# A masked softmax bound by DMA: the first store waits for the last whole load

**Chip and metric.** One core of one Trainium2 chip. The metric is the device time of one execution in microseconds (us). All runs compared here are with a granted clock of 1.0.

## The reference

For each of 16 batches, a softmax over the last axis of 8 x 256 rows, of which only the first `length` columns count; the others become 0. Lengths lie between 128 and 255. The reference, shortened:

```python
# x: (16, 8, 256, 256) float32, lengths: (16,) int32
for b in range(batch):
    masked = x[b, :, :, :lengths[b]]
    masked = masked - np.max(masked, axis=-1, keepdims=True)
    e = np.exp(masked)
    result[b, :, :, :lengths[b]] = e / np.sum(e, axis=-1, keepdims=True)
```

## The kernel before

A batch is 2 MB: 128 partitions of 16 rows of 256 floats, so 16 KB contiguous per partition. There are eight slots in SBUF. SyncE loads batches 0 to 3 whole. GpSimd (POOL in the profile) loads batches 4 to 15, each only as wide as its length needs (widths in steps of 8 columns from 160 to 240, or all 256). VectorE (DVE) clips the columns past the length (the clip uses `len_s`, the bounds on all partitions), ScalarE (ACT) exponentiates and sums, DVE divides, and SyncE stores in pieces. All stores and the four whole loads go through SyncE's queue, called q1 in the profile; GpSimd's loads go through q0.

```python
for h in range(2):                                   # SyncE: batch 0 in two halves
    s = slice(h * half, (h + 1) * half)
    nc.sync.dma_start(out=xt[:, 0, s], in_=x_f[0, :, s]).then_inc(s_ld[h], 16)
nc.scalar.dma_start(out=word64, in_=lengths[None, :]).then_inc(s_word, 16)
for b in range(1, ahead):                            # ahead = 4: batches 1 to 3
    nc.sync.dma_start(out=xt[:, b], in_=x_f[b]).then_inc(s_ld[b + 1], 16)
for b in range(batch):
    for s in parts(b):                               # pieces of a batch: halves and quarters, late ones whole
        nc.sync.wait_ge(s_out, 2 * b + (s.stop - 1) // half + 1)
        # ... (from batch 2 on: an earlier store of the same parity is done)
        nc.sync.dma_start(out=out_f[b, :, s, :], in_=xt[:, b % slots, s, :]) # ...
# ...
nc.gpsimd.dma_start(out=word64_p, in_=lengths[None, :]).then_inc(s_word_p, 16)
# ...
nc.gpsimd.wait_ge(s_v, 1)
for b in range(ahead, slots):                        # the fills: zeros past column 160
    nc.gpsimd.memset(xt[:, b, :, low:], 0.0).then_inc(s_fill, 1)
nc.gpsimd.wait_ge(s_word_p, 16)
nc.gpsimd.wait_ge(s_fill, slots - ahead)
nc.gpsimd.wait_ge(s_ld[ahead - 1], 16)               # GpSimd's gate: batch 2 has landed
with nc.Fori(0, (batch - ahead) // 2, 1, engines=[POOL]) as q:
    # ... two narrow loads a turn: length to a register, branches to its width, issue
```

The softmax here doesn't subtract the row's maximum and nothing guards it: scores larger than these inputs give would overflow.

Of the kernel before, what the change touches and what calls it, by code (L numbers as in the profile page):

```python
# [11 lines left out]
I32 = mybir.dt.int32  # L12
# [4 lines left out]
POOL = mybir.EngineType.Pool  # L17
# [3 lines left out]
def kernel(  # L21
# [6 lines left out]
    nc = tc.nc  # L28
    P = nc.NUM_PARTITIONS

    batch, heads, seq_q, seq_k = x.shape
# [10 lines left out]
    ahead = 4  # L42
# [7 lines left out]
    def parts(b):  # L50


        if b < 10:
            cuts = [0, half, half + quarter, nt]
        elif b < 12 or b == batch - 1:
            cuts = [0, half, nt]
        else:
            cuts = [0, nt]
        return [slice(i, j) for i, j in zip(cuts, cuts[1:])]

    pool = ctx.enter_context(tc.tile_pool(name="all", bufs=1))
    psum = ctx.enter_context(tc.tile_pool(name="psum", bufs=1, space=bass.MemoryType.PSUM))
    xt = pool.tile([P, slots, nt, seq_k], F32, name="xt")
    word64 = pool.tile([1, batch], mybir.dt.int64, name="word64")
    word = word64.bitcast(I32)
    word64_p = pool.tile([1, batch], mybir.dt.int64, name="word64_p")
    word_p = word64_p.bitcast(I32)
    len_b = pool.tile([1, batch], BF16, name="len_b")
    ones = pool.tile([1, P], BF16, name="ones")
    len_f = psum.tile([P, batch], F32, name="len_f")  # L70
# [8 lines left out]
    with tc.tile_critical(no_gpsimd_drain=True):  # L79
        sem = lambda n: ctx.enter_context(nc.semaphore(n))  # L80
        s_word = sem("s_word")
        s_word_p = sem("s_word_p")
        s_ones = sem("s_ones")
        s_lenb = sem("s_lenb")
        s_lenf = sem("s_lenf")
        s_ld = [sem(f"s_ld{k}") for k in range(ahead + 1)]
# [6 lines left out]
        s_v = sem("s_v")  # L93
# [4 lines left out]
        def length(engine, at):  # L98

            return nc.values_load(  # L100
                at,
                engines=[engine],
                skip_runtime_bounds_check_because="compared with constants, never an address",
            )


        for h in range(2):
            s = slice(h * half, (h + 1) * half)
            nc.sync.dma_start(out=xt[:, 0, s], in_=x_f[0, :, s]).then_inc(s_ld[h], 16)  # L109
        nc.scalar.dma_start(out=word64, in_=lengths[None, :]).then_inc(s_word, 16)  # L110
        for b in range(1, ahead):
            nc.sync.dma_start(out=xt[:, b], in_=x_f[b]).then_inc(s_ld[b + 1], 16)  # L112
        for b in range(batch):
            s_b = s_st[b % 2]
            for s in parts(b):
                nc.sync.wait_ge(s_out, 2 * b + (s.stop - 1) // half + 1)
                if b >= 2 and s.start == 0:
                    nc.sync.wait_ge(s_b, 64 * (b // 2 + 1))
                nc.sync.dma_start(
                    out=out_f[b, :, s, :], in_=xt[:, b % slots, s, :]  # L120
                ).then_inc(s_b, 16 * ((s.stop - s.start) // quarter))
# [5 lines left out]
        def pick(v, n, slot, par, ws):  # L127

            if len(ws) == 1:
                w = ws[0]  # L130
                nc.gpsimd.dma_start(  # L131
                    out=xt[:, slot, :, :w], in_=x_n[:, n, :, :w]
                ).then_inc(s_sw[par], 16)
                return
            m = (len(ws) - 1) // 2
            with nc.gpsimd.If(v <= ws[m]):  # L136
                pick(v, n, slot, par, ws[: m + 1])
            with nc.gpsimd.Else():
                pick(v, n, slot, par, ws[m + 1 :])
# [3 lines left out]
            iota_i, pattern=[[1, seq_k]], base=0, channel_multiplier=0  # L143
        ).then_inc(s_iota, 1)
        nc.gpsimd.memset(ones, 1.0).then_inc(s_ones, 1)  # L145
        nc.gpsimd.dma_start(out=word64_p, in_=lengths[None, :]).then_inc(s_word_p, 16)  # L146
        for par in range(2):
            nc.gpsimd.memset(seed[:, par : par + 1], 0.0).then_inc(s_st[par], 64)  # L148
        nc.gpsimd.wait_ge(s_v, 1)
        for b in range(ahead, slots):  # L150
            nc.gpsimd.memset(xt[:, b, :, low:], 0.0).then_inc(s_fill, 1)  # L151
        nc.gpsimd.wait_ge(s_word_p, 16)
        nc.gpsimd.wait_ge(s_fill, slots - ahead)
        nc.gpsimd.wait_ge(s_ld[ahead - 1], 16)
        with nc.Fori(0, (batch - ahead) // 2, 1, engines=[POOL]) as q:  # L155
            for par in range(2):
                n = 2 * q + (ahead + par)
                v_len = length(POOL, word_p[0:1, bass.ds(2 * n, 1)])
                with nc.gpsimd.If(q >= 1):  # L159
                    nc.gpsimd.wait_ge(s_sw[par], 16 * q)  # L160
                    nc.gpsimd.wait_ge(s_st[par], 64 * q)  # L161
                pick(v_len, bass.ds(n, 1), bass.ds(n % slots, 1), par, widths + [seq_k])
# [9 lines left out]
        def step(ins):  # L172
# [8 lines left out]
                out=down, in0=iota_i, scalar1=0.5, scalar2=-big, op0=ALU.add, op1=ALU.mult  # L181
# [7 lines left out]
                out=len_s, in0=len_f, scalar1=big, scalar2=None, op0=ALU.mult  # L189
# [56 lines left out]
        with nc.Fori(0, 2 * batch, 1, engines=[ACT]) as i:  # L246
            nc.scalar.wait_ge(s_min, i + 1)
            at = bass.ds(i % (2 * slots), 1)
            for j in range(half):
                e = x_h[:, at, j, :]  # L250
                ins = nc.scalar.activation(  # L251
                    out=e, in_=e, func=EXP, accum_out=sum_h[:, bass.ds(i, 1), j]
# [32 lines left out]
```

## Time and profile before

| | before |
|---|---|
| time, median of the first 3 runs | 157.06 us (156.97 to 157.08) |
| span of the profiled run | 155.5 us |
| bytes moved | 62.08 MB |
| DVE, ACT busy | 77%, 68% |

The lines that carry the reading are in the prediction below. In short: the 16 DMA engines are busy from 2 us to about 153 (9 tenths in every slice but the first and the last), so a change counts by the DMA time that it wastes or saves. A row of the view of stretches has the stretch and its length in us, the busy time and count of PE, PEld, DVE, ACT and POOL, the granted clock, the DMA share and the GB/s moved.

```profile
2.00:36.00 34.00, 0.17 (x1) 0.10 (x1) 29.88 (x20) 24.41 (x119) 7.61 (x9) 1.00 1.00 402
```

### The profile page before, as it was taken

To read this page: it belongs to the slowest core of one execution; us is meant where nothing else is said; L and a number is where in the kernel's file an instruction comes from. 1 tells how busy PE (TensorE), PEld (TensorE's weight loads), DVE (VectorE), ACT (ScalarE), POOL (GpSimd) and SP (SyncE) were. 2 spreads that over 40 slices of the span, in tenths; PEclk is the share of its full clock that TensorE was granted. 3 is DMA by queue.
4 is the path that set the end of the run, shared out by engine and by line. 5 is a ranking of instruction groups with operands and counts; after the bars stand their busy time and mean duration, and the time that the engine had idled before them with its cause. 6 is when DMAs were issued, how large, how long until landed. Compare 5 with 4: busy or idle time off the path is not lost.

```text
span 155.5 us, 1320 instructions
## 1 busy us (share of the span) xinstructions
PE 0.2 (0%) x1; PEld 0.1 (0%) x1; DVE 120.0 (77%) x84; ACT 105.1 (68%) x514; POOL 19.4 (12%) x26
## 2 busy tenths in 40 slices
PE   0000000000000000000000000000000000000000
PEld 0000000000000000000000000000000000000000
DVE  4963999999999968939895999997977999920000
ACT  3029599999989893956969298989592989400000
POOL 7900031003020202002020202020100000000000
DMA  4999999999999999999999999999999999999991
GB/s 116 428 443 426 434 312 388 416 442 427 393 395 410 415 416 406 420 410 413 409 412 419 402 417 406 415 411 405 425 421 432 420 419 432 457 426 422 415 434 61
DMA packets 10452, 62.08 MB, mean 399 GB/s; under 512 B 930, under 2 KB 1026, under 8 KB 7122
## 3 DMA queue, kind: packets, MB, share of 16 engines
q1 hardware_dynamic: 6336, 41.95, 65.9%
q0 software_dynamic: 4112, 20.12, 32.0%
q14 instruction: 2, 0.02, 0.0%
q10 hardware_dynamic: 2, 0.00, 0.0%
HBM read 28.51 MB, written 33.55 MB: 399 GB/s over the span
## 4 chain that ended last, share of the span: by engine, by line
DMA 67%; DVE 11%; issue 6%; POOLq 2%; SPq 1%; POOL 0%; DVEq 0%
DMA xt<-in_x_dram 60%; DVE xt L224 7%; DMA out_dram<-xt 7%; DVE xt L197 3%; POOLq L100 1%; POOLq L136 1%; POOLq L131 1%; SPq L109 1%; DVE inv_sum L221 0%; POOL xt L131 0%; SPq L112 0%; POOLq L159 0%; POOLq L155 0%; DVEq L214 0%; POOLq L161 0%
## 5 line engine op out<-in xcount | busy, mean ns | idle before, releaser
L251 ACT ACTIVATE xt<-xt x256 | 102.4, 402 | 27.2 <-DVE xt L197 27.2
L224 DVE TENSOR_TENSOR xt<-xt,inv_sum 128x2048 f32<-128x2048 f32 x32 | 73.3, 2292 | 1.1
L251 ACT ACTIVATION_READ_ACCUMULATOR xt<-xt x256 | 48.2, 188 | 0.0
L197 DVE SCALAR_TENSOR_TENSOR xt<-down,len_s,xt 128x2048 f32<-128x2048 f32 (+1 forms) x17 | 37.7, 2222 | 11.1 <-DMA xt<-in_x_dram 10.2
L131 POOL DMA_DIRECT2D xt<-in_x_dram x12 | 12.7, 1057 | 89.7 <-issue 45.7
L221 DVE RECIPROCAL inv_sum<-row_sum 128x8 f32<-128x8 f32 x32 | 6.2, 195 | 2.4 <-ACT xt L251 2.4
L185 DVE CAST len_b<-word 1x16 bf16<-1x16 int32 x1 | 5.6, 5595 | 0.4 <-DMA word<-in_lengths_dram 0.4
L151 POOL MEMSET xt<- 128x1536 f32 x4 | 5.3, 1392 | 0.0
L243 ACT ACT_TABLE_LOAD x1 | 1.3, 1283 | 1.6 <-SPq L79 1.6
L180 DVE TENSOR_SCALAR down<-iota_i 128x256 f32<-128x256 int32 x1 | 0.3, 295 | 1.6 <-POOL iota_i L142 1.6
L146 POOL DMA_DIRECT2D word_p<-in_lengths_dram x1 | 0.6, 643 | 0.1
L188 DVE TENSOR_SCALAR len_s<-len_f 128x16 f32<-128x16 f32 x1 | 0.2, 174 | 0.4 <-PE len_f L167 0.4
L142 POOL IOTA iota_i<- 128x256 int32 x1 | 0.3, 331 | 0.6 <-SPq L79 0.6
L243 ACT ACTIVATE warm<-const-float32-0.0 128x1 f32<-128x1 f32 x1 | 0.2, 203 | 0.0
L145 POOL MEMSET ones<- 1x128 bf16 x1 | 0.2, 194 | 0.0
L167 PE MATMUL len_f<-len_b,ones 1*128 1x16 bf16 x1 | 0.2, 168 | 8.0 <-DVE len_b L185 8.0
L269 POOL MEMSET const-float32-0.0<- 128x1 f32 x1 | 0.1, 98 | 0.3 <-issue 0.3
L148 POOL MEMSET seed<- 1x1 f32 x2 | 0.1, 88 | 0.0
L167 PEld LDWEIGHTS len_f<-len_b,ones 1*128 1x128 bf16 x1 | 0.1, 98 | 8.0 <-issue 8.0
L269 POOL MEMSET const-float32-1.0<- 128x1 f32 x1 | 0.1, 98 | 0.0
L269 POOL MEMSET const-bfloat16-1.0<- 128x1 bf16 x1 | 0.1, 98 | 0.0
L269 POOL MEMSET const-uint8-127<- 128x1 uint8 x1 | 0.1, 98 | 0.0
(1 smaller groups left out, 0.0 us busy)
## 6 DMA issues: line engine op xcount, KB each, us to landing
out_dram<-xt SPq DMA_DIRECT2D x16, 1024.0 KB
out_dram<-xt SPq DMA_DIRECT2D x20, 512.0 KB
xt<-in_x_dram SPq DMA_DIRECT2D x3, 2048.0 KB, 16.0
out_dram<-xt SPq DMA_DIRECT2D x3, 2048.0 KB
xt<-in_x_dram POOLq DMA_DIRECT2D x3, 1728.0 KB, 15.9
xt<-in_x_dram POOLq DMA_DIRECT2D x2, 2048.0 KB, 16.0
xt<-in_x_dram POOLq DMA_DIRECT2D x2, 1600.0 KB, 14.5
xt<-in_x_dram POOLq DMA_DIRECT2D x2, 1280.0 KB, 13.6
```

Source lines behind the costliest of these rows:

```text
L100: return nc.values_load(at, engines=[engine], skip_runtime_bounds_check_because="compared with constants, never an address",)
L109: nc.sync.dma_start(out=xt[:, 0, s], in_=x_f[0, :, s]).then_inc(s_ld[h], 16)
L131: nc.gpsimd.dma_start(out=xt[:, slot, :, :w], in_=x_n[:, n, :, :w]).then_inc(s_sw[par], 16)
L136: with nc.gpsimd.If(v <= ws[m]):
L146: nc.gpsimd.dma_start(out=word64_p, in_=lengths[None, :]).then_inc(s_word_p, 16)
L151: nc.gpsimd.memset(xt[:, b, :, low:], 0.0).then_inc(s_fill, 1)
L185: nc.vector.tensor_copy(out=len_b, in_=word[:, ::2]).then_inc(s_lenb, 1)
L197: return nc.vector.scalar_tensor_tensor(out=t, in0=down[:, None, lo:hi].to_broadcast([P, s.stop - s.start, hi - lo]), scalar=len_s[:, b : ...
L221: step(nc.vector.reciprocal(out=inv_sum[:, b, s], in_=row_sum[:, b, s]))
L224: nc.vector.tensor_tensor(out=t, in0=t, in1=inv_sum[:, b, s, None].to_broadcast([P, half, seq_k]), op=ALU.mult,).then_inc(s_out, 1)
L243: nc.scalar.activation(out=warm, in_=nc.const_aps.tensor(0.0, (P, 1), F32), func=EXP)
L251: ins = nc.scalar.activation(out=e, in_=e, func=EXP, accum_out=sum_h[:, bass.ds(i, 1), j])
```

## The change

Its intent: let the whole loads have the DMA engines to themselves, and let GpSimd's narrow loads be open before the first store is. In passing, GpSimd reads the lengths from the copy that ACT's queue fetches, and the fills wait until DVE has made the bounds. The diff, shortened:

```diff
-        nc.scalar.dma_start(out=word64, ...)         # moved ahead of the loads; same queue of ACT
+        nc.sync.wait_ge(s_ld[ahead], 16)             # ahead of the loop of stores: the hold
-        nc.gpsimd.dma_start(out=word64_p, ...)       # and word64_p, s_word_p with it
-        nc.gpsimd.wait_ge(s_v, 1)
+        nc.gpsimd.wait_ge(s_v, 2)                    # fills after the bounds
-        nc.gpsimd.wait_ge(s_word_p, 16)
+        nc.gpsimd.wait_ge(s_word, 16)
-                v_len = length(POOL, word_p[...])
+                v_len = length(POOL, word[...])
```

More of the change, by code (lines that the diff above doesn't have):

```diff
@@ L65 @@
     word = word64.bitcast(I32)
-    word64_p = pool.tile([1, batch], mybir.dt.int64, name="word64_p")
-    word_p = word64_p.bitcast(I32)
     len_b = pool.tile([1, batch], BF16, name="len_b")
@@ L81 @@
         s_word = sem("s_word")
-        s_word_p = sem("s_word_p")
         s_ones = sem("s_ones")
@@ L104, in length @@
             )
+        nc.scalar.dma_start(out=word64, in_=lengths[None, :]).then_inc(s_word, 16)
         for h in range(2):
@@ L109 @@
             nc.sync.dma_start(out=xt[:, 0, s], in_=x_f[0, :, s]).then_inc(s_ld[h], 16)
-        nc.scalar.dma_start(out=word64, in_=lengths[None, :]).then_inc(s_word, 16)
         for b in range(1, ahead):
             nc.sync.dma_start(out=xt[:, b], in_=x_f[b]).then_inc(s_ld[b + 1], 16)
+        nc.sync.wait_ge(s_ld[ahead], 16)
         for b in range(batch):
@@ L145 @@
         nc.gpsimd.memset(ones, 1.0).then_inc(s_ones, 1)
-        nc.gpsimd.dma_start(out=word64_p, in_=lengths[None, :]).then_inc(s_word_p, 16)
         for par in range(2):
             nc.gpsimd.memset(seed[:, par : par + 1], 0.0).then_inc(s_st[par], 64)
-        nc.gpsimd.wait_ge(s_v, 1)
+        nc.gpsimd.wait_ge(s_v, 2)
         for b in range(ahead, slots):
             nc.gpsimd.memset(xt[:, b, :, low:], 0.0).then_inc(s_fill, 1)
-        nc.gpsimd.wait_ge(s_word_p, 16)
+        nc.gpsimd.wait_ge(s_word, 16)
         nc.gpsimd.wait_ge(s_fill, slots - ahead)
@@ L157 @@
                 n = 2 * q + (ahead + par)
-                v_len = length(POOL, word_p[0:1, bass.ds(2 * n, 1)])
+                v_len = length(POOL, word[0:1, bass.ds(2 * n, 1)])
                 with nc.gpsimd.If(q >= 1):
```

## The prediction

Its sum came to +0.85 us, and so to 157.9 us. Three figures in it are estimates and not readings of a trace: the 0.1 us of the cast, the 0.2 us for the start, and the chance of one in two.

> **What bounds the kernel now.** I read the page first, for what is full. Its line of slices says that DMA is.
>
> ```profile
> span 155.5 us, 1320 instructions
> ...
> DMA  4999999999999999999999999999999999999991
> GB/s 116 428 443 426 434 312 388 416 442 427 393 395 410 415 416 406 420 410 413 409 412 419 402 417 406 415 411 405 425 421 432 420 419 432 457 426 422 415 434 61
> ...
> q1 hardware_dynamic: 6336, 41.95, 65.9%
> q0 software_dynamic: 4112, 20.12, 32.0%
> ```
>
> Every slice but the first and last is at 9 tenths, while DVE is busy 77% of the span and ACT 68%. Queue q1 carries SyncE's four whole loads and all stores (41.95 MB), q0 GpSimd's narrow loads (20.12 MB). The kernel moves 62.08 MB whatever the order, so its time is bytes over rate, plus every stretch in which the 16 engines move nothing. One slice stands out: the sixth, 19.4 to 23.3 us, at 312 GB/s. The view of stretches cuts it finer; the last two columns are the DMA share and GB/s.
>
> ```profile
> 4.00:20.00 16.00, 0.17 (x1) 0.10 (x1) 12.31 (x9) 7.28 (x36) 3.87 (x3) 1.00 1.02 433
> 20.00:21.00 1.00, 0.00 (x0) 0.00 (x0) 1.00 (x1) 1.00 (x7) 0.28 (x1) 1.00 1.34 426
> 21.00:22.00 1.00, 0.00 (x0) 0.00 (x0) 1.00 (x2) 1.00 (x6) 0.92 (x1) 1.00 1.19 279
> 22.00:23.00 1.00, 0.00 (x0) 0.00 (x0) 1.00 (x1) 1.00 (x7) 0.00 (x0) 1.00 0.57 197
> 23.00:24.00 1.00, 0.00 (x0) 0.00 (x0) 0.97 (x3) 1.00 (x6) 0.51 (x1) 1.00 0.73 270
> 44.00:116.00 72.00, 0.00 (x0) 0.00 (x0) 62.91 (x45) 57.79 (x286) 8.67 (x9) 1.00 1.02 412
> 123.00:147.00 24.00, 0.00 (x0) 0.00 (x0) 13.85 (x10) 10.34 (x52) 0.00 (x0) 1.00 1.02 433
> ```
>
> Pure loads run at 433, the mixture of narrow loads and stores at 412, pure stores at 433. From 21 to 24 the three rows sum to 0.746 MB where 433 GB/s would have moved 1.299: 0.553 MB, or 1.3 us, is lost there. I call this **the dip**. Compute has no say at the end: the last DVE operation starts at 134.7 and takes 2.3 us, and stores go on to about 153.
>
> Who holds whom at the changeover is in the timeline (start, duration, engine, line) and in the DMA view of 24.0 to 25.5 and 25.5 to 27.0 us.
>
> ```profile
> 2.30 5.59 DVE L185 CAST len_b<-word 1x16 bf16<-1x16 int32 x1 [0.40 <-DMA word<-in_lengths_dram]
> 2.54 5.33 POOL L151 MEMSET xt<- 128x1536 f32 x4
> 9.29 2.48 DVE L197 SCALAR_TENSOR_TENSOR xt<-down,len_s,xt 128x1024 f32<-128x1024 f32 x2 [0.87 <-DVE len_s L188]
> 16.73 19.80 SPq L119 DMA_DIRECT2D out_dram<-xt  x9
> 20.71 1.20 POOL L131 DMA_DIRECT2D xt<-in_x_dram  x1 [12.85 <-issue]
> ```
>
> ```profile
> q1 hardware_dynamic: 75, 0.61, 98.5%
> ```
>
> ```profile
> q1 hardware_dynamic: 77, 0.37, 59.5%
> q0 software_dynamic: 48, 0.23, 37.1%
> ```
>
> The first store is issued at 16.73, but batch 3, the last whole load, lands only at 24.2 (issued at 3.3, longest landing 20.9 us). From 16 to 19 us the DMA view counts 95 packets, 16 of them tiny, and 1.29 MB: 16 KB a packet, the size of a whole load's row. From 24.0 to 25.5 it is 0.61 MB in 75 packets, 8 KB each, the row of a half store. So the early store did not share the engines with batch 3; it stood behind it and followed without a gap. No q0 packet shows before 25.5, though GpSimd issued at 20.71: its first narrow load needed about 5 us to open. At the changeover it is thus the queued stores that keep the engines fed.
>
> [...] Here the first load, issued at 1.13, shows data at 2.1, which is 1.0 us; and GpSimd's took 5 us. [...] a cast of 1x16 elements takes 5.59 us and ends with the four fills.
>
> **The change part by part.**
>
> *Fills after the bounds.* `word` has landed at 2.30; without fills beside it I expect the cast to take some 0.1 us, and matmul and scaling (0.17 and 0.17 us, with the 0.35 us wait between cast and scaling seen now) to end near 3. The fills (5.33 us) move to about 3.0 to 8.4, still far from GpSimd's gate on batch 2 at 18.5. The first clip can start when batch 0's first half is there (issue 1.13 plus 5.1, the shortest landing: 6.2) instead of 9.29: up to 3 us earlier for DVE and ACT. On the path: nothing, for the stores stand behind batch 3 anyway.
>
> *Lengths shared.* It removes one GpSimd issue (0.64 us) and a few bytes of DMA, both ahead of a 10 us idle stretch of GpSimd: 0 on the path. One doubt: DMA is also slow from 2 to 4 us (246 GB/s, where 433 would be 0.75 MB more in 2 us). Most of that is start-up, but the removed DMA is issued just then; if it does harm, up to half a microsecond comes back.
>
> *The hold.* SyncE now issues its first store only after batch 3's semaphore. Loads before it do not go faster, as no store was among them. After it comes a **hole**: semaphore at 24.2, issue some 0.05 us later (DVE ended at 16.70 and SyncE issued at 16.73 in the old trace), 1.0 us to data: about 25.3. GpSimd's gate (batch 2) and its way to the issue are unchanged, so q0 opens near 25.3 to 25.7 and doesn't fill it. What the old kernel moved of stores before 25.3: from 21 to 24 the view counts 58 large packets and 0.75 MB, which is 34 of 16 KB and 24 of 8 KB, so 0.20 MB of stores; from 24.0 to 25.3 it is 1.3 us of 0.415 MB, 0.54 MB. Together 0.74 MB, at 433 GB/s **1.7 us**, and no later stage can win it back, since the engines are full to the end. The backlog at the release is no problem: with compute earlier, batch 0 and half of batch 1 are ready by then.
>
> *The dip.* This I can't place from one trace. It starts 0.4 us after GpSimd's first narrow issue (20.71) and lasts past the store issues at 21.4 and 21.8, so either may be its cause. If it is GpSimd's opening, it stays; if it is stores standing in the same ring behind reads, the hold takes it away and wins 1.3 us back.
>
> Sum: +1.7 for the hole, minus 1.3 times one chance in two, minus some 0.2 for the start: +0.85 us, so 157.9.
>
> **Rivals.**
>
> 1. *The hole is filled by narrow loads.* The intent: GpSimd is open when SyncE stops. For it: its gate passes 5.7 us before batch 3 lands[...]. Against it: 2.2 us of register work and branches to the issue, and 5 us to the first packet. If q0 opened by 23.9, there would be no hole: 156.9 with the dip, 155.6 without.
> 2. *The dip stays, and the hole comes on top*, with no gain at the start: 158.8. For it: the dip begins before the stores of 21.4 are issued, and the one of 16.73 did no harm for four microseconds. Against it: GpSimd's later issues, 36.24 or 87.15, come with no dip (403 GB/s from 87 to 91).
> 3. *DVE becomes the bound after the release*, as stores start late and slots come free later. From 24 to 44 us DVE is busy nearly all the time. Against it: it starts up to 3 us earlier, the narrow loads pace themselves one behind the other, and the stores end 15 us after the last compute. Worth under 0.5 us.
> 4. *The hold lets more loads be pure* and saves on the mixture (412 against 433). Against it: those rates go with small packets and not with direction, and no packet changes its size: 0.
>
> **Range and chances.** Dip gone, start better, hole partly filled: 156.3. Dip kept, hole whole, and a second stumble of half a microsecond to a microsecond at the release: 159.6. Faster by 2% would need 153.9, that is the dip, the whole start-up loss and more, with no hole: 3 in 100. Slower by 2% would need 160.2, twice the hole: 4 in 100. Within 2%: 93 in 100.
>
> **What would show it.** Right: the cast near 0.1 us and the first clip near 6.3; the first store issued just after batch 3 lands; no packets, or very few, for 1 to 2 us after that; rates of 412 and 433 in the same later stages; an end shifted by the same amount. It is wrong if narrow packets show before batch 3 has landed, if loads of batch 3 land much earlier than 24.2 less the dip, or if the later mixture runs at another rate than 412. If the dip is at the same place, GpSimd's opening is its likely cause; if it is gone, the queued stores.

## The result, and the profile after

The changed kernel takes 157.84 us (median of 4 runs, 157.59 to 158.22), the kernel before 157.01 in the same rounds. The ratio is 1.0055, with a 95% interval of 1.0034 to 1.0076: the same within 2%, but slower beyond the noise. A ratio here is the mean time of one kernel's fast runs over that of the other's of the same rounds, so not quite the ratio of the medians.

The page after, its span and its two DMA lines in 40 slices:

```profile
span 155.9 us, 1320 instructions
...
DMA  4999989999999999999999999999999999999992
GB/s 109 425 450 433 420 341 287 407 434 414 405 395 419 408 424 404 412 417 402 420 415 411 411 403 419 406 415 414 415 445 421 411 429 431 441 425 446 414 427 105
```

There are now two low slices, 341 and 287, where one stood at 312. The stretches after:

```profile
2.00:4.00 2.00, 0.17 (x1) 0.10 (x1) 0.34 (x2) 1.13 (x2) 0.95 (x1) 1.00 0.96 238
4.00:20.00 16.00, 0.00 (x0) 0.00 (x0) 11.04 (x8) 10.04 (x50) 4.38 (x4) 1.00 1.01 432
...
22.00:23.00 1.00, 0.00 (x0) 0.00 (x0) 1.00 (x1) 1.00 (x7) 0.05 (x1) 1.00 0.56 161
23.00:24.00 1.00, 0.00 (x0) 0.00 (x0) 0.97 (x3) 1.00 (x6) 0.56 (x1) 1.00 0.81 197
24.00:25.00 1.00, 0.00 (x0) 0.00 (x0) 1.00 (x1) 1.00 (x7) 0.00 (x0) 1.00 0.94 360
25.00:26.00 1.00, 0.00 (x0) 0.00 (x0) 1.00 (x2) 1.00 (x6) 0.00 (x0) 1.00 1.06 326
26.00:27.00 1.00, 0.00 (x0) 0.00 (x0) 1.00 (x1) 1.00 (x7) 0.00 (x0) 1.00 0.99 211
27.00:28.00 1.00, 0.00 (x0) 0.00 (x0) 1.00 (x1) 1.00 (x6) 0.00 (x0) 1.00 0.97 298
...
2.00:36.00 34.00, 0.17 (x1) 0.10 (x1) 27.21 (x22) 27.18 (x132) 8.34 (x7) 1.00 0.99 391
```

Batch 3's loads now run undisturbed to 22 us (432 GB/s from 4 to 20 us, 442 from 20 to 22). Then two low stretches follow each other. From 22 to 24 us, 0.358 MB moves where 433 GB/s would move 0.866: 1.2 us lost. From 24 to 28, 1.195 MB instead of 1.732: 1.2 us lost. Between them, at 360, is the recovery from one and the start of the other. Over 2 to 36 us the rate falls from 402 to 391 GB/s; 11 GB/s over 34 us is 0.37 MB, which at the 416 GB/s of the later part (36 to 152 us: 416 before, 417 after) is 0.9 us. The whole loss sits here: the measured difference of the medians is 0.83.

Who moves in the low stretches? The timeline after, and the DMA view (packets, MB, share of the 16 engines) of 24 to 27 and of 27 to 28 us:

```profile
2.30 0.16 DVE L182 CAST len_b<-word 1x16 bf16<-1x16 int32 x1 [0.39 <-DMA word<-in_lengths_dram]
3.05 5.33 POOL L148 MEMSET xt<- 128x1536 f32 x4 [1.11 <-DVE len_s L185]
6.47 1.28 DVE L194 SCALAR_TENSOR_TENSOR xt<-down,len_s,xt 128x1024 f32<-128x1024 f32 x1 [3.48 <-DMA xt<-in_x_dram]
20.75 1.29 POOL L129 DMA_DIRECT2D xt<-in_x_dram  x1 [12.37 <-issue]
23.55 3.45 SPq L117 DMA_DIRECT2D out_dram<-xt  x6
```

```profile
q0 software_dynamic: 187, 0.90, 99.4%
```

```profile
q0 software_dynamic: 40, 0.19, 71.5%
q1 hardware_dynamic: 13, 0.11, 25.1%
```

The cast fell from 5.59 to 0.16 us and the first clip starts at 6.47 instead of 9.29. (That clip ran beside the fills, which took from 3.05 to 8.38, and still in 1.28 us; in the kernel before, clips of that size took 1.28 us after the fills had ended. So the fills held up the cast and not the clip; why, the traces do not show.) SyncE issues the first store at 23.55, once batch 3 has landed. But from 24 to 27 us all the data that moves is GpSimd's: 0.90 MB by q0 alone, at 299 GB/s. The first store packets, 13 of 8 KB, come after 27: 3.5 us after the issue.

### The profile page after: what moved, and what is told of

Its sections match the earlier page's. It is cut to its first block, busy times and chain, and to the rows that moved or that the text cites. A ratio compares the mean times of both kernels' runs of the same rounds, so it can differ in the third digit from the quotient of the medians.

```text
span 155.9 us, 1320 instructions
## 1 busy us (share of the span) xinstructions
PE 0.2 (0%) x1; PEld 0.1 (0%) x1; DVE 115.0 (74%) x84; ACT 105.1 (67%) x514; POOL 19.0 (12%) x25
## 4 chain that ended last, share of the span: by engine, by line
DMA 70%; DVE 8%; issue 5%; POOLq 2%; SPq 1%; POOL 0%; DVEq 0%
DMA xt<-in_x_dram 70%; DVE xt L221 6%; DVE xt L194 2%; POOLq L134 1%; POOLq L129 1%; POOLq L97 1%; SPq L107 1%; POOL xt L129 0%; DVE inv_sum L218 0%; SPq L109 0%; POOLq L156 0%; POOLq L152 0%; POOLq L158 0%; POOLq L136 0%; DVEq L211 0%
## 5 line engine op out<-in xcount | busy, mean ns | idle before, releaser
L182 DVE CAST len_b<-word 1x16 bf16<-1x16 int32 x1 | 0.2, 164 | 0.4 <-DMA word<-in_lengths_dram 0.4
```

## The experiments

Theory at the start (A): the hold makes the whole change, and the old dip belonged to stores queued behind loads. Rival (B): the dip belongs to GpSimd's opening of its narrow loads, and the loss comes in part from the other edits. Each run kept the results correct.

**One part alone.** The hold alone, on the kernel before:

```diff
+        nc.sync.wait_ge(s_ld[ahead], 16)
         for b in range(batch):
```

> The kernel before plus the hold alone. Theory A (the hold makes the whole change): 157.8 us, +0.8 against the kernel before, batch 3 lands near 23.5 with no dip in its loads, first store data near 27. Theory B (part of the loss comes from sharing the lengths or moving the fills): at most +0.4, 157.0 to 157.4.

Measured: 158.16 us, ratio 1.0081 (1.0067 to 1.0095); its rates of 22 to 24 and 24 to 28 us are low as in the changed kernel, 220 and 298 GB/s (there 179 and 299). The other two edits alone (the changed kernel, this line removed):

```diff
-        nc.sync.wait_ge(s_ld[ahead], 16)
```

> The changed kernel without the hold. Theory A: the time of the kernel before within 0.3 us, 156.7 to 157.3, and the dip from 21 to 24 us is back in batch 3's loads. Theory B: 157.4 or more. If the early compute alone were of use: below 156.7.

Measured: 156.85 us, ratio 1.0007 (0.9991 to 1.0022), with the dip from 20 to 24 us back (287 GB/s). So the hold is the cause; sharing the lengths and moving the fills are worth nothing that the interval can show. Whether they save some 0.3 us under the hold (158.16 against 157.84, in different rounds) is not settled; the first 34 us give no support (393 GB/s with the hold alone, 391 with all three).

**Is the dip GpSimd's?** The kernel before, with GpSimd's gate one load later:

```diff
-        nc.gpsimd.wait_ge(s_ld[ahead - 1], 16)
+        nc.gpsimd.wait_ge(s_ld[ahead], 16)
```

> The kernel before with GpSimd's first narrow load gated on batch 3 instead of batch 2; no hold. If the dip from 21 to 24 us comes of stores queued behind loads, whatever GpSimd does, it stays where it is and batch 3 lands at 24.2. If it needs GpSimd's opening, batch 3's loads run at 433 to their end, it lands near 23.0 to 23.5, and a dip shows 1 to 4 us later, in the stores. Time: 156.5 to 157.3 either way, lower if the dip is gone for good (155.8).

Measured: 157.34 us, ratio 1.0026 (1.0006 to 1.0046; the profiled execution was a slow one of its kind, 158.87). Its timeline and its row of 20 to 24 us:

```profile
27.32 1.20 POOL L131 DMA_DIRECT2D xt<-in_x_dram  x1 [19.45 <-issue]
```

```profile
20.00:24.00 4.00, 0.00 (x0) 0.00 (x0) 3.97 (x4) 4.00 (x22) 0.00 (x0) 1.00 0.91 305
```

The dip is at its place (305 GB/s) although GpSimd issues nothing before 27.32. GpSimd's opening is not its cause. A second, smaller low follows when the narrow loads come: 364 GB/s from 30 to 32 us.

**Is it the short rows?** The changed kernel, with GpSimd's first load made at full width (16 KB rows, 0.46 MB more to move):

```diff
+                with nc.gpsimd.If(q >= 1):
                     pick(..., widths + [seq_k])
+                with nc.gpsimd.Else():
+                    pick(..., [seq_k])
```

> The changed kernel, where GpSimd's first narrow load (batch 4, 1.6 MB in rows of 800 bytes) is made at full width (2.0 MB in rows of 16 KB); 0.46 MB or 1.06 us more to move, the result is the same. If the slow stretch from 22.5 to 28 us (some 270 GB/s while GpSimd's load has the engines alone) comes of the short rows, it runs at 430 and the sum is 157.8 - 2.2 + 1.1, 156.7 or less. If any first load of GpSimd is that slow, the stretch stays and the time is 158.9.

Measured: 158.93 us, ratio 1.0131 (1.0110 to 1.0151), with both low stretches still there:

```profile
22.00:24.00 2.00, 0.00 (x0) 0.00 (x0) 1.97 (x3) 2.00 (x11) 0.53 (x1) 1.00 0.73 274
24.00:28.00 4.00, 0.00 (x0) 0.00 (x0) 4.00 (x2) 4.00 (x22) 0.00 (x0) 1.00 0.96 299
```

The short rows are not the reason; the second stretch is as slow as with them, and the time rises by the extra bytes (158.93 against 157.84 us, in different rounds; 0.46 MB at 433 GB/s is 1.06 us).

**Nothing open at all.** The changed kernel with GpSimd also gated on batch 3 (the same edit as above):

> The changed kernel, with GpSimd's first narrow load also gated on batch 3, so that after the hold nothing is open. If the hold costs what is opened into empty engines, the gap after batch 3 is now a real hole of 1.0 to 1.3 us, with store data from about 24.6, then the narrow loads open later beside stores and cost little; time 157.8 to 158.6. If the slow stretch before store data is tied to the first store and comes wherever the store opens, it is there with no reads to suffer from it, and the time is no worse than the changed kernel's 157.8.

Measured: 159.68 us, ratio 1.0159 (1.0130 to 1.0187), worse than either expectation. The two rows that tell it:

```profile
22.00:24.00 2.00, 0.00 (x0) 0.00 (x0) 1.97 (x3) 2.00 (x12) 0.00 (x0) 1.00 0.08 33
...
28.00:33.00 5.00, 0.00 (x0) 0.00 (x0) 4.93 (x5) 5.00 (x27) 0.56 (x1) 1.00 1.02 323
```

Here is the hole that I had predicted for the changed kernel, and its size shows what a store costs when nothing runs: issued at 23.41, its data begins at 24.25, 0.84 us later and with no dip. Then GpSimd issues at 25.65, and from 28 to 33 us, where its narrow loads are to join the running stores (none of their packets shows from 28 to 32), the rate falls to 323 GB/s. So a low stretch comes both when stores join running loads (305 GB/s with GpSimd's gate alone) and when loads join running stores. Its size differs: 1.3 us here, where stores and narrow loads meet for the first time, but some 0.4 us from 28 to 33 us in the run with GpSimd's gate alone (397 GB/s), where stores had met batch 3's loads already.

**Is it a first-time cost?** The changed kernel without the hold, plus a store of 64 KB at about 2 us into rows of the last batch, from ACT's queue; SyncE waits for it before it stores that batch:

```diff
+        nc.scalar.wait_ge(s_iota, 1)
+        nc.scalar.dma_start(out=out_f[batch - 1, :, 0, 0:mid], in_=iota_i.bitcast(F32)[:, 0:mid]).then_inc(s_warm, 16)
```

> The changed kernel without the hold, plus a small store of 64 KB that ACT's queue issues at about 2 us into rows that the last batch overwrites later (0.15 us of bytes). If the dip ahead of the first store data is paid once, when the first store of the program runs, it moves to the start and batch 3's loads run at 433 to their end: 155.9 to 156.4. If it is paid where a queue goes over from loads to stores, it stays from 20.5 to 24 us: 157.0.

Measured: 157.15 us, ratio 0.9994 (0.9972 to 1.0016). The same store in SyncE's own queue, between batch 0 and batch 1 (`nc.sync` in place of `nc.scalar`):

> The same small store, issued by SyncE in its own queue between batch 0 and batch 1. If the first store of this queue pays, the dip moves to about 5 to 8 us and is gone from 20.5 to 24: no gain in time unless it is smaller for a small store (156.0 to 157.1). If each change from loads to stores in the queue pays by what is stored, both places show it: 157.0 to 158.0.

Measured: 157.06 us, ratio 1.0002 (0.9971 to 1.0033). In both, the dip stays (322 and 303 GB/s from 20 to 24 us), and the small store itself leaves no visible one (438 and 436 GB/s from 5 to 9 us). So it isn't a cost that any first store pays once for the program or for the queue. These runs leave open that a larger store would have paid it: the small one joined running loads for nothing.

**Where does it sit?** The changed kernel without the hold, with the first half of batch 0 stored from ACT's queue, so that it stands behind no load:

```diff
+        # ACT: the first two turns of its loop peeled off, then (SyncE leaves this part out)
+        nc.scalar.wait_ge(s_out, 1)
+        nc.scalar.dma_start(out=out_f[0, :, 0:half, :], in_=xt[:, 0, 0:half, :]).then_inc(s_st[0], 32)
```

> The changed kernel without the hold, with the first store (half of batch 0, 1 MB) issued from ACT's queue at about 14 us instead of standing behind the loads in SyncE's. If queues take turns on the engines, 8 KB packets of it show from about 15 us beside batch 2's loads, which land up to 2.4 us later, and the time stays at 156.9. If the dip belongs to the opening of the stores it moves to 14 to 17 us; if it belongs to the end of the loads it stays at 20.5 to 24.

Measured: 156.45 us, ratio 0.9948 (0.9920 to 0.9976). The issue in its timeline, and its stretches:

```profile
13.67 0.41 ACTq L251 DMA_DIRECT2D out_dram<-xt  x1
```

```profile
15.00:18.00 3.00, 0.00 (x0) 0.00 (x0) 2.97 (x3) 1.55 (x8) 0.00 (x0) 1.00 0.98 330
20.00:24.00 4.00, 0.00 (x0) 0.00 (x0) 3.97 (x3) 4.00 (x22) 1.29 (x1) 1.00 0.97 412
```

The dip moved with the store, to 15 to 18 us. It is also cheaper: (433 - 330) x 3 / 433 is 0.7 us. The DMA view finds no packet of this store before 17.6 us, so it took 4 us to show data although its queue was empty. The expectation's turns between the queues were not seen in these 4 us: from 14 to 17.6 us the view counts 85 packets of SyncE's queue and none of ACT's (q10), from 17.6 to 19 us 30 and 29.

By now the theory (C in what follows) was: a stream that joins a running one costs about 1 us; the kernel before has its stores and its narrow loads join in one go, and the hold makes two of it.

**Size of the first piece.** Batch 0 stored in four quarters instead of a half and two quarters, no hold:

```diff
-        if b < 10:
+        if b == 0:
+            cuts = [0, quarter, half, half + quarter, nt]
+        elif b < 10:
```

> The changed kernel without the hold, batch 0 stored in four quarters (4 KB rows, 0.5 MB each) in place of a half and two quarters. Theory C (a stream that joins a running one costs about 1 us once, whatever its first piece) gives the dip at 20 to 24 us of some 1.1 us and 156.9 us. If the dip grows with the size of the first store's rows (512-byte rows of a small store showed none), it halves and the time is 156.3 to 156.6.

Measured: 156.97 us, ratio 1.0007 (0.9985 to 1.0029), with 307 GB/s from 20 to 24 us, where the run without the hold has 287. Halving the rows does not halve the dip.

**A shorter hold.** The changed kernel, where SyncE waits for batch 2:

```diff
-        nc.sync.wait_ge(s_ld[ahead], 16)
+        nc.sync.wait_ge(s_ld[ahead - 1], 16)
```

> The changed kernel with the hold one load earlier: SyncE waits for batch 2 (18.5 us) instead of batch 3. Theory C: the stores are again in the queue behind batch 3, open together with the narrow loads in one dip, and the time is that of the kernel before within 0.3 us, ratio 0.998 to 1.002. If holding as such costs (compute ahead of stores, backlog), 157.3 or more.

Measured: 156.97 us, ratio 1.0003 (0.9985 to 1.0021).

```profile
20.00:24.00 4.00, 0.00 (x0) 0.00 (x0) 3.93 (x5) 4.00 (x22) 1.72 (x2) 1.00 0.91 283
24.00:28.00 4.00, 0.00 (x0) 0.00 (x0) 4.00 (x2) 4.00 (x22) 0.13 (x1) 1.00 0.99 412
```

One dip, then full speed, as in the kernel before. Here holding was free: the stores still stood in the queue behind a load when the loads ended.

**Loads beside loads.** No hold, and GpSimd gated on batch 0:

```diff
-        nc.gpsimd.wait_ge(s_ld[ahead - 1], 16)
+        nc.gpsimd.wait_ge(s_ld[1], 16)
```

> The changed kernel without the hold, GpSimd gated on batch 0 (8.7 us) instead of batch 2: its narrow loads join SyncE's loads near 11 us, reads beside reads, and the stores join later, near 20 to 30 us. If any queue that joins costs about 1 us, there are two dips, one from 11 to 15 and one before the first store data, and the time is 157.7 to 158.2. If only stores joining loads (or loads joining stores) cost, there is one dip and the time is 156.9 or a little more.

Measured: 156.90 us, ratio 1.0001 (0.9979 to 1.0023).

```profile
14.00:18.00 4.00, 0.00 (x0) 0.00 (x0) 3.97 (x3) 2.06 (x11) 0.00 (x0) 1.00 0.98 414
...
23.00:26.00 3.00, 0.00 (x0) 0.00 (x0) 2.93 (x4) 2.82 (x15) 0.00 (x0) 1.00 0.94 330
```

GpSimd issues at 11.00; from 11 to 15.5 us the rate is 431 GB/s, and when its packets come it goes over to that of a mixture, with no dip. The dip comes later, where the stores join. So it is not any second queue that costs, but stores and loads coming together.

Does every such meeting cost? The trace of the changed kernel says no. From 37.7 to 38.9 us its narrow loads pause, and stores have the engines to themselves, at 423 GB/s (first line, the DMA view of that stretch; q1 has 111 packets in it). The next narrow load, issued at 34.08, then joins the running stores, with no dip (second line):

```profile
q0 software_dynamic: 1, 0.00, 0.0%
```

```profile
36.00:41.00 5.00, 0.00 (x0) 0.00 (x0) 4.96 (x4) 5.00 (x27) 0.76 (x1) 1.00 0.99 412
```

With GpSimd shut until 27 us, the second meeting cost 0.4 us. In every run the first lasting meeting cost 0.7 to 1.4 us, by the same sum against 433 GB/s (330 GB/s over 3 us with ACT's store, 283 over 4 us with the shorter hold). So theory C holds for that one, and not for each that follows.

**An attempt at a better version.** The first store on ACT's queue, with GpSimd gated on batch 1, so that both open together:

```diff
-        nc.gpsimd.wait_ge(s_ld[ahead - 1], 16)
+        nc.gpsimd.wait_ge(s_ld[ahead - 2], 16)
```

> The version with the first store on ACT's queue (156.45 against 157.25 beside it), with GpSimd gated on batch 1 instead of batch 2, so that its narrow loads open near 16 us together with that store. Theory C: one dip of about 0.9 us near 15 to 18, no other, same time as that version, ratio about 0.995. If GpSimd's opening costs on its own, 0.5 to 1 us more.

Measured: 156.69 us, ratio 0.9992 (0.9973 to 1.0010), with the one dip expected (336 GB/s from 15 to 18 us) and none from 20 to 24 us (434 GB/s), but without the gain; GpSimd's first issue falls between 15 and 18 us. The version with ACT's store alone has an interval below 1, some 0.5%; as its near twin does not, I do not call it established.

## Why the prediction was right or wrong

The time was right: 157.84 where 157.9 stood, and well inside the range. That it was so near is luck: the hold does cost, but all three terms of the sum were wrong and made up for each other. One of the prediction's own signs of being wrong came, too: narrow packets showed at about 22.8 us, before the last packets of SyncE's queue (22.9, tiny ones; its last of 16 KB came by 22.3) and SyncE's release (23.55). The few packets that it wanted for 1 to 2 us after the release were 0.90 MB of narrow loads from 24 to 27 us. Point by point:

- **Lengths shared: right.** 0, and the doubt about the start fell too: 238 GB/s from 2 to 4 us, where 246 was before. So the removed DMA was not what makes that stretch slow; what does, no run shows.
- **Fills after the bounds: right.** The cast took 0.16 us with no fill beside it (5.59 before), the first clip began at 6.47, and none of it is in the time, as the run without the hold shows.
- **"After it comes a hole": right that the hold costs, wrong in how.** I took two sizes from single cases: 1.0 us from a store's issue to its data, and 5 us for GpSimd's opening. In the changed kernel GpSimd's data came at about 22.8, some 2 us after its issue, just as batch 3 ran out; there was a gap of 0.45 us (22.3 to 22.75 us: 9 packets, 0.00 MB) and not the hole of 1 us or more. And the store took 3.5 us. The 1.0 us holds when nothing runs (0.84 measured with both gates closed), not beside loads (3.5 and 4 us). The time from issue to data of GpSimd's first narrow load was 5.2 us in the kernel before and 4.5 us with its gate on batch 0 (11.00 to 15.5), both beside other data, and 2.0 us in the changed kernel, where batch 3 ran out beside it.
- **Rival 1, narrow loads fill the hole: half right.** They were open, but they moved little at first: 179 GB/s over 22 to 24 us, 1.2 us lost to a start into drained engines. They opened before the 23.9 that I had asked for, yet the time was not the 156.9 that should have followed.
- **Rival 2, the dip stays and the hole comes on top (158.8): near in kind, too dear.** There are two losses, but of 1.2 us each where 1.7 and 1.3 stood.
- **The dip, "one chance in two": both readings fell.** It is not GpSimd's opening (it stays when GpSimd is shut until 27 us), and the hold does not remove it. It goes with the coming together of stores and loads, wherever that is: 20 to 24 us before, 24 to 28 after, 15 to 18 with ACT's store. The hold moved it from batch 3's loads into GpSimd's.
- **The sum** was thus right by luck, with other terms. Predicted: +1.7 for the hole, -0.65 for the dip, -0.2 for the start. Measured against 433 GB/s from 20 to 28 us: after, 1.2 us for the narrow loads' start on their own and 1.2 for the dip in its new place, together 2.4; before, 1.3 for the dip (293 GB/s from 20 to 24 us) and 0.2 for the ordinary mixture behind it (410 GB/s from 24 to 28), together 1.5. The difference is +0.9: what stood for the hole was too large, and the two savings that were to lower it did not come. The step that failed is the latency that I took for fixed: the first data of a store came after 0.84 to 4 us and that of a first narrow load after 2.0 to 5.2 us, with what was in flight, and the dip goes with it.
- **Rival 3 (DVE as the bound) and rival 4 (purer stretches): rightly set aside.** The later stage (36 to 152 us) runs at 416 and 417 GB/s. That the rates go with small packets and not with direction, the trace before bears out: loads and stores together ran at 430 GB/s from 34 to 38 us, where 15 of 149 packets are under 8 KB, and at 412 from 44 to 116 us, where 5489 of 6514 are.

What stays open: why the engines slow down for about 3 us (249 GB/s from 21 to 24 us in the kernel before) before, or around, the first data of the joining kind. The runs exclude GpSimd's opening as the cause of the old dip, short rows, and a first-time cost that a 64 KB store would pay, and tie it to the first lasting meeting of stores and loads, in either order. They do not say what the engines do in that time, nor whether the first meeting costs because it is the first: no run was made for that. No run lets narrow loads go alone with no store issued, so it is also not shown that the low stretch from 24 to 28 us of the changed kernel needs the stores. And why the narrow loads of the kernel before join its stores for free is not shown by a run of its own.

## What to carry to other kernels

In this kernel, bound by DMA, a store queued behind loads was not in their way: it was what kept the engines fed when the loads ended (415 GB/s from 24.0 to 25.5 us, 98.5% of the engines' time in q1; 157.01 us against 157.84 with the hold, and 156.97 in its own rounds with the shorter hold). In a kernel like it, let the store be queued there, or hold it only so long that it still stands behind a load. Then look in the trace for a stream that starts on drained engines, and for the place where stores and loads first come together. Here each cost 1.2 us in the changed kernel, the hold put one after the other, and later meetings cost 0 to 0.4 us.
